# One list-schedule item for each marked group of small matmuls in a hybrid decoder layer

## The chip, the core and the metric

The kernel runs on one core of a Trainium2 chip. The metric is the device time of one execution in microseconds (us); a kernel's time is the median of its runs.

The engines are named as in the profile: PE is the matmul engine (PEld its weight loads), DVE, ACT and POOL are the vector, scalar and general engines, SP issues nearly all DMAs.

## The reference

One decoder layer over 4096 tokens of width 1024. The input is normalised and modulated, one projection feeds three mixers side by side, and their gated outputs go through one output projection:

```python
h = _rmsnorm(x, g_pre) * (1.0 + scale[:, None]) + shift[:, None]
proj = h @ w_in
...
attn = _sliding_window_attention(aq..., ak..., av..., sinks)   # 8 query heads, 2 kv heads, window 128
attn = attn * jax.nn.silu(ag)
...
rwkv = _rwkv7_mixer(h, rr, rk, rv, ...) * jax.nn.silu(rg)      # 4 heads of 64, delta-rule state per head
gla = _gla_mixer(h, gq, gkk, gv, gk1, gk2, gk_b, gla_norm_w) * jax.nn.silu(gg)   # 4 heads, key 32, value 64
y = jnp.concatenate([attn, rwkv, gla], axis=-1) @ w_out
return x + gate[:, None] * _rmsnorm(y, g_post)
```

RWKV and GLA are recurrences over the tokens, done in chunks: inside a chunk they are products of small matrices, and from chunk to chunk a state is carried.

## The kernel before

The 4096 tokens are cut into 16 slabs of 256. The program has two stages.

Stage one computes h, RWKV and GLA of all slabs, in generators that follow each slab: `a` (h), `p` (projections; their PSUM tiles are `pv`, `lp`, `zz`, `gqk`), `w` (decays and the a-lora `aps`), `qa` (RWKV scores: PSUM tiles `atp`, evacuated by DVE into `AT`), `qb` (scores go through DRAM, `adr`, into `AS`, and DVE solves small triangles step by step in `tsc` and `TT`), `qc` (small triangular products `Xp`, `Xq`, `X2`), `q2` (the RWKV state, four chunks one after the other: `rp`, `up`, `sp`, `yp`, then `yt`), `v`, `k` (transposes `kp`), `r` (GLA: scores `gap`, output `op`, state `kvp`) and `c` (weights split for stage two). Slab i+1 overlaps slab i, except where the state forces the order.

Stage two computes attention, gates and output projection of all slabs: `qkv` (`kp`, `qp`, `vp`), `gates` (`gp`), `s` (attention: scores `sc`, softmax on ACT and DVE, probabilities `pr` transposed on DVE, values `ovp`), `m` and `outp` (output projection, again tiles called `op`). A short stretch between the two stages (first slab's projections and attention) isn't ordered by hand.

Most matmuls use the whole 128x128 array. The small ones use a part of it and several can be in the array at once: 64x64 for `atp`, `gap`, `aps`, `rp`, `up` and half of `yp`, 128x64 for the GLA `op`, `sp` and the other half of `yp`, 32x64 for `ovp`, 32x32 for the triangles. The shape is called the tiling here. A matmul of fp32 data is two records of PE in the trace.

What sets the order: the generators run first only to record. A class `Order` notes every instruction (`note`) with the tiles that it reads and writes, and `pin` then simulates the engines with a table of costs, picks one ready instruction after the other and pins this order on each engine. A step becomes ready when the steps that it `needs` have ended, and those whose `turn` comes first (PSUM and SBUF buffers of one tag are handed out in the order of the program) have started. Among ready steps the lowest `rank` goes first (its place in the program); on PE a step of another tiling is passed over for up to `TILING_WAIT` when one of the present tiling is ready:

```python
            if e == "PE" and mode is not None and steps[k].array[0] != mode:

                same = [q for q in at if steps[q].array[0] == mode]
                wait = max(now - ready[e][q] for q in at if steps[q].array[0] != mode)
                if same and (mode != (4, 4) or wait < TILING_WAIT):
                    k = same[0]
```

So each matmul of a small product is an item of its own, and a product can be taken in pieces with other work between them.

PSUM has eight banks. The scores `atp` and `gap` use the banks of the tags `at` and `mq` (one buffer each), the GLA `op` uses `at`, the four `ovp` tiles use `tr`, `m`, `y` and `mq`.

All operations are issued through one helper, so that every instruction of the profile has its line: L320 in this kernel, L330 in the changed one, whose file is longer above it. Groups are told apart by their tiles.

Of the kernel before, what the change touches and what calls it, by code (L numbers as in the profile page):

```python
# [58 lines left out]
class Step:  # L59


    __slots__ = ("ins", "eng", "occ", "lat", "table", "array", "bytes", "half", "rank", "needs", "turn", "start", "end", "left", "then")


class Order:
# [1 line left out]


    def __init__(self, tc):
        self.tc, self.held, self.masks, self.lag, self.urgent = tc, {}, {}, 0, 0  # L70
        self.steps = []
        self.wrote, self.read, self.users, self.slots, self.known = {}, {}, {}, {}, set()

# [25 lines left out]
    def note(self, eng, name, outs, ins, func, r):  # L99

        st = Step()
        st.ins, st.eng, st.table, st.array, st.bytes, st.then = r.ins, str(eng.engine).split(".")[-1], None, None, 0, []
        st.half, st.rank = None, len(self.steps) + self.lag
        e, o = st.eng, outs[0]
        on_psum = [a for a in ins if str(a.tensor.space) == "PSUM"]
# [110 lines left out]
    def pin(self):  # L216

        steps = self.steps
        ready = {e: {} for e in ENGINES}
        for k, st in enumerate(steps):  # L220
            st.left = len(st.needs) + len(st.turn)
            for j in [*st.needs, *st.turn]:
                steps[j].then.append(k)
            if not st.left:
                ready[st.eng][k] = 0.0
        free = dict.fromkeys(ENGINES, 0.0)
        cells, mode, table, pipe, half = [0.0] * 16, None, None, 0.0, {}
        last = {}
        for _ in steps:
            e = min((e for e in ENGINES if ready[e]), key=lambda e: max(free[e], min(ready[e].values())))  # L230
            now = max(free[e], min(ready[e].values())) + 1e-9
            at = sorted((k for k, t in ready[e].items() if t <= now), key=lambda k: (steps[k].rank, k))
            k = at[0]
            if e == "PE" and mode is not None and steps[k].array[0] != mode:

                same = [q for q in at if steps[q].array[0] == mode]
                wait = max(now - ready[e][q] for q in at if steps[q].array[0] != mode)
                if same and (mode != (4, 4) or wait < TILING_WAIT):
                    k = same[0]
            st, t = steps[k], max(free[e], ready[e].pop(k))  # L240
            if e == "PE":
                m, at, passes, took, issue = st.array
                if mode is not None and m != mode:
                    t = max(t, max(cells)) + 0.094
                mode = m
                t = max(t, max(cells[c] for c in at))
                for c in at:
                    cells[c] = t + passes * took
                free[e], st.end = t + issue * passes, t + passes * took + 0.165
            else:  # L250
                if st.half is not None:
                    was, half[e] = half.get(e, st.half), st.half
                    if was[0] != st.half[0] or None not in (was[1], st.half[1]) and was[1] != st.half[1]:
                        t = max(t, free[e] + 0.115)
                if st.table is not None and st.table != table:
                    t, table = max(t, free[e] + 1.28), st.table
                free[e], st.end = t + st.occ, t + st.lat
                if st.bytes:

                    pipe = max(pipe, t + 1.7) + st.bytes / 310e3  # L260
                    st.end = max(st.end, pipe)
            st.start = t
            if e in last:
                self.tc.add_manual_dep(
                    st.ins, last[e], mybir.DependencyInfo(mybir.DependencyClass.NoSync, mybir.DependencyReason.DATA))
            last[e] = st.ins.name
            for q in st.then:
                to = steps[q]
                to.left -= 1
                if not to.left:  # L270
                    at = max([steps[j].start for j in to.turn], default=0.0)
                    for j, data in to.needs.items():
                        by = steps[j]
                        if by.eng != to.eng:
                            at = max(at, by.end + HOP_FROM[by.eng] + HOP_INTO.get(to.eng, 0.0))
                        elif to.eng == "SP":
                            at = max(at, by.end + 0.05)
                        elif to.eng != "PE" and data:
                            at = max(at, by.end + 0.03)
                    ready[to.eng][q] = at  # L280
        self.forget()


# [100 lines left out]
def hybrid_kernel(ctx, tc, x, vecs, rows, adaw, w1, wl, w2, wo, w2aug, a2, gk2, cst, ctr, ctg, abias, out):  # L384
# [92 lines left out]
    def mt(name):  # L477
        return pst("m", name)
# [43 lines left out]
            yield  # L522

    E = [dict() for _ in range(NS)]

# [98 lines left out]
    with ExitStack() as p1:  # L626
# [477 lines left out]
        def stage_d(i):  # L1104
# [39 lines left out]
            for b in range(2):  # L1144
# [4 lines left out]
                S.activation(em[:, b].rearrange("p c n -> p (c n)"), cw[:, :260], AF.Exp, scale=-1.0)  # L1149
                yield ["m"]  # L1150
            aps = mt("aps")
            for b in range(2):
                for h in range(2):
                    PE.matmul(aps[64 * h : 64 * h + 64, b * NT : (b + 1) * NT],
                              a2s[64:128, b * P + 64 * h : b * P + 64 * h + 64], x1[64:128, :], start=True, stop=True)
            ta = wt([P, 2, NT], "ta")
            e["ta"] = ta
            for b in range(2):
# [10 lines left out]
        def stage_qa(i):  # L1169
# [56 lines left out]
            corners = ((0, 0), (0, 1), (1, 0), (1, 1))  # L1226
            for g in range(2):
                aps_ = [pst(tag, "atp").rearrange("p (a b n) -> p a b n", a=2, b=2) for tag in ("at", "mq")]
                for c2 in range(2):
                    for b in range(2):  # L1230
                        for s, hb in corners:
                            c = 2 * g + c2
                            PE.matmul(aps_[hb][half[hb ^ s], c2, b, :], KB[half[hb], b, c, s, :],
                                      RA[half[hb], b, c].rearrange("p s n -> p (s n)"), start=(c2 == 0 and b == 0),
                                      stop=(c2 == 1 and b == 1))
                for hb in range(2):
                    V.tensor_tensor(AT[:, hb, 2 * g : 2 * g + 2], aps_[hb],
                                    rmask.rearrange("p (a b n) -> p a b n", a=1, b=1).to_broadcast([P, 2, 2, P]),
                                    op=ALU.mult)
                yield ["at", "mq"]  # L1240
# [101 lines left out]
        def stage_r(i):  # L1342
# [15 lines left out]
            for a in range(2):  # L1358
                yield [qb[a], "at", "mq"]
                gap = [pst(tag, "gap")[:, 0:NT] for tag in ("at", "mq")]  # L1360
                for hk in half:
                    for hp, sl in enumerate(half):
                        PE.matmul(gap[hp][hk], kg[sl, a, hk], qb[a][sl, 2 * hp : 2 * hp + 2, :].rearrange("p h n -> p (h n)"),
                                  start=True, stop=True)

                for hp in range(2):
                    V.tensor_tensor(qb[a][:, 2 * hp : 2 * hp + 2, :], gap[hp].rearrange("p (h n) -> p h n", h=2),
                                    gmask.rearrange("p (o n) -> p o n", o=1).to_broadcast([P, 2, P]), op=ALU.mult)
            yield [kt, "mq"]
            osb = wt([P, 2, NT], "osb", 1)  # L1370
            for a in range(2):
# [7 lines left out]
                V.scalar_tensor_tensor(Gn, Gn, egp[:, a, 128:129], bdm, op0=ALU.mult, op1=ALU.mult)  # L1379
                yield [Gc, qb[a], "at"]  # L1380
                op_ = pst("at", "op")
                for ht in half:
                    PE.matmul(op_[ht, :NT], qg[:, a, ht], Gc, start=True, stop=False)
                for h in range(4):
                    for ht in half:
                        PE.matmul(op_[ht, h * 64 : h * 64 + 64], qb[a][:, h, ht], vg[:, a, h * 64 : h * 64 + 64],
                                  start=False, stop=(h == 3))
                S.copy(osb[:, a, :], op_[:, :NT])
                yield [Gn, "mq"]
            osq = cs2([P, 2, NT], "osq")  # L1390
# [265 lines left out]
    def stage_s(i):  # L1656
# [8 lines left out]
        for a in range(2):  # L1665
# [48 lines left out]
            ov = [pst(tag, "ovp")[:, 0:P].rearrange("p (j n) -> p j n", j=4) for tag in tags]  # L1714

            lo = 4 if first else 0
            for d in range(5):
                for n in range(4):
                    if n + d < lo:
                        continue  # L1720
                    vt_, z = vblk[a + (n + d) // 4], (n + d) % 4
                    for kv in range(2):
                        PE.matmul(ov[n][kv * 64 : kv * 64 + 64], vt_[32 * n : 32 * n + 32, z, kv * 64 : kv * 64 + 64],
                                  pT[kv][32 * n : 32 * n + 32, :, 32 * (n + d) : 32 * (n + d) + 32],
                                  start=(n + d == max(lo, n)), stop=(d == 4))
            for n in range(4):
                S.copy(mx[:, 0:4, a * P + 32 * n : a * P + 32 * n + 32], ov[n])
            yield ["at", "sq"]
# [329 lines left out]
```

## Time and profile before

| | |
|---|---|
| runs | 2148.49, 2153.25, 2159.01 us; median 2153.25 |
| profiled execution | 2150.68 us, its span 2148.7 us, mean granted PE clock 0.985 |
| PE | 94% busy, 24311 matmul records |
| DVE | 76% busy, ACT 53%, POOL 9% |
| DMA | 241.90 MB, mean 113 GB/s |

Stage one ends at about 1120 us of the span, the stretch between the stages at about 1190 us, and stage two takes the rest. A busy PE in the page counts records that overlap, so the start of a record and the start of the next one tell more than their lengths.

### The profile page before, as it was taken

The numbers are of one execution on the slowest core, as the hardware profiler recorded it, in microseconds if no ns is written. First come the engines' busy times: TensorE is split into PE (matmuls) and PEld (weight loads), VectorE is DVE, ScalarE is ACT, GpSimd is POOL, SyncE is SP. The second block draws the span as 40 slices with busy tenths as digits, with TensorE's granted clock in tenths as the row PEclk, the third lists the DMA queues.
The fourth block names the chain that finished last, engine by engine and source line by source line (L and its number), as shares of the span: only waits on it lengthen the run. The fifth ranks groups of instructions, "written<-read, shape, count | busy, mean of one in ns | idle before, by whom it ended". The sixth has DMA issues, their size and how long they took to land. (4 is left out here: it accounts for less than half of the span.)

```text
span 2148.7 us, 60377 instructions
## 1 busy us (share of the span) xinstructions
PE 2025.3 (94%) x24311; PEld 1577.1 (73%) x24311; DVE 1630.7 (76%) x5204; ACT 1142.8 (53%) x2739; POOL 203.5 (9%) x404
## 2 busy tenths in 40 slices
PE   4999999999999999989888999999999999999996
PEld 4787788877787877777667667777777777777773
DVE  6687777678677789876765888777778877778876
ACT  3966676567776667654324444434344444444442
POOL 0010111111111111112600000000000000000000
PEclk9999999999999999999989999999999999999998
DMA  9232333133313224423415343433343333334341
GB/s 313 94 108 81 97 99 96 35 100 108 114 62 106 75 71 122 124 75 96 145 59 179 122 160 105 134 105 111 114 135 121 121 121 111 111 120 141 109 133 69
DMA packets 187249, 241.90 MB, mean 113 GB/s; under 512 B 52160, under 2 KB 145874, under 8 KB 182740
## 3 DMA queue, kind: packets, MB, share of 16 engines
q1 hardware_dynamic: 185220, 236.76, 34.4%
q8 instruction: 194, 3.18, 0.6%
q10 hardware_dynamic: 1744, 1.21, 0.2%
q14 instruction: 91, 0.75, 0.1%
HBM read 177.08 MB, written 60.82 MB: 111 GB/s over the span
## 5 line engine op out<-in xcount | busy, mean ns | idle before, releaser
L320 PEld LDWEIGHTS <-mtp 128*128 128x128 f16 x1344 | 130.8, 98 | 144.0 <-issue 5.3
L320 PE MATMUL op<-o,mtp 128*128 128x512 f16 x768 | 174.2, 380 | 0.0
L320 ACT ACTIVATE pr<-pr,nm,lsc 128x256 f32<-128x256 f32 (+1 forms) x256 | 149.7, 591 | 37.1 <-DVE nm L320 37.1
L320 PE MATMUL op<-ov,mtp 128*128 128x512 f16 x576 | 146.1, 383 | 2.3 <-ACT mtp L320 2.1
L320 PEld LDWEIGHTS <-hT 128*128 128x128 f16 x1536 | 116.6, 98 | 22.0 <-issue 4.2
L320 DVE TENSOR_TENSOR yv<-op,yv 128x512 f32<-128x512 f32 x112 | 75.3, 683 | 57.7 <-PE op L320 42.5
L320 DVE CUSTOM_DVE_ANT_0 pr<-sc,ab,sinks 128x256 f32<-128x256 f32 (+1 forms) x256 | 108.0, 476 | 14.4 <-PE sc L320 8.0
L320 ACT ACTIVATE mtp<-yv,oi 128x1024 f16<-128x1024 f32 x32 | 36.7, 1147 | 126.1 <-DVE yv L320 124.6
L320 ACT ACTIVATE ag<-gp,gh 128x512 f32<-128x512 f32 x64 | 43.7, 683 | 112.2 <-PE gp L320 112.2
L320 PE MATMUL pv<-gvh,hT 128*128 128x272 f16 x512 | 98.6, 282 | 1.1 <-DVE hT L320 1.0
L320 PE MATMUL gqk<-hT,gqkh 128*128 128x256 f16 x512 | 91.1, 277 | 4.8 <-DVE zb L320 4.8
L320 DVE SCALAR_TENSOR_TENSOR ag<-ag,gp 128x512 f32<-128x512 f32 x64 | 43.8, 684 | 68.1 <-ACT ag L320 68.1
L320 POOL COPY kT<-kT 128x512 f16<-128x512 f16 x15 | 9.9, 657 | 890.5 <-DVE kT L320 890.5
L320 PE MATMUL zz<-hT,kh 128*128 128x256 f16 x512 | 93.5, 273 | 0.0
L320 PE MATMUL qp<-hT,q1h 128*128 128x256 f16 x512 | 88.9, 278 | 4.0 <-DVE kT L320 4.0
L320 PE MATMUL lp<-hT,Lh 128*128 128x256 f16 x512 | 91.5, 276 | 0.4 <-ACT vg L320 0.2
L320 PE MATMUL zz<-hT,rh 128*128 128x256 f16 x512 | 90.1, 277 | 0.0
L320 PE MATMUL zz<-hT,vh 128*128 128x256 f16 x512 | 87.2, 273 | 0.8 <-DVE zb L320 0.8
L320 PE MATMUL gp<-hT,q3h 128*128 128x256 f16 x512 | 86.9, 274 | 0.1
L320 PE MATMUL qp<-hT,q0h 128*128 128x256 f16 x512 | 86.5, 275 | 0.4 <-DVE yv L320 0.4
L320 PE MATMUL gp<-hT,q5h 128*128 128x256 f16 x512 | 86.8, 273 | 0.0
L320 PE MATMUL gp<-hT,q4h 128*128 128x256 f16 x512 | 85.0, 273 | 0.0
(428 smaller groups left out, 6155.3 us busy)
## 6 DMA issues: line engine op xcount, KB each, us to landing
ov<-woscr SPq DMA_DIRECT2D x96, 512.0 KB, 4.3
xt<-in_x SPq DMA_DIRECT2D x16, 1024.0 KB, 5.1
hscr<-hT SPq DMA_DIRECT2D x16, 1024.0 KB, 5.5
hT<-hscr SPq DMA_DIRECT2D x16, 1024.0 KB, 4.8
out<-yv SPq DMA_DIRECT2D x32, 512.0 KB, 2.9
x<-in_x SPq DMA_DIRECT2D x30, 512.0 KB, 4.2
cs<-in_w SPq DMA_DIRECT2D x112, 128.0 KB, 2.3
v<-vscr SPq DMA_DIRECT2D x128, 64.0 KB, 3.4
```

Of the source, the lines that this page charges most:

```text
L320: r = f(*args, **kw)
```

## The change

The kernel marks five groups of matmuls with a number (`joint()` ... `joint(False)`): the a-lora `aps` (4 matmuls), each half of the RWKV scores `atp` (16), each half of the GLA scores `gap` (4), each GLA output `op` (10), and the attention values `ovp` (40). `note` stores the number in the step. In `pin`, neighbours on PE with one number and one tiling form a burst: its first member is its head, all outer needs and turns of the members count against the head, and when the head is picked all members are issued one behind the other. Everything else of `pin` keeps its rules (readiness is now summed as steps end, in `left` and `when`). No instruction of the program is added or taken away; the loads of ACT's function tables, which follow from the order, go from 65 to 67 in the built program.

```diff
+        bursts, head = {}, list(range(len(steps)))
         for k, st in enumerate(steps):
-            st.left = len(st.needs) + len(st.turn)
+            if st.eng == "PE":
+                h = head[k - 1] if k else 0
+                if k and steps[h].eng == "PE" and st.joint and st.joint == steps[h].joint and st.array[0] == steps[h].array[0]:
+                    head[k] = h
+                bursts.setdefault(head[k], []).append(k)
+        left, when = [0] * len(steps), [0.0] * len(steps)
+        for k, st in enumerate(steps):
             for j in [*st.needs, *st.turn]:
-                steps[j].then.append(k)
-            if not st.left:
+                if head[j] != head[k]:
+                    left[head[k]] += 1
+                    steps[j].then.append(k)
+        for k, st in enumerate(steps):
+            if head[k] == k and not left[k]:
                 ready[st.eng][k] = 0.0
...
-            st, t = steps[k], max(free[e], ready[e].pop(k))
-            if e == "PE":
...
+            first = max(free[e], ready[e].pop(k))
+            for k in bursts.get(k, [k]):
+                st, t = steps[k], max(first, free[e])
+                if e == "PE":
...
+    burst = itertools.count(1)
+
+    def joint(on=True):
+        model.order.joint = next(burst) if on else 0
...
             lo = 4 if first else 0
+            joint()
             for d in range(5):
...
                                   start=(n + d == max(lo, n)), stop=(d == 4))
+            joint(False)
```

How the order moves is shown at three places. The first is PE in stage two, within the gates of a slab (`gp` from the weights `q5h` and `q5l`): the attention values `ovp` of half a slab. In the kernel before, four of the 40 matmuls stand alone:

```order
L320 MATMUL gp<-hT,q5h 128x256
L320 MATMUL ovp<-pr,v_24378 64x128 x4
L320 LDWEIGHTS q5l
L320 MATMUL gp<-hT,q5l 128x256
L320 LDWEIGHTS q5h
```

and the other 36 follow seven `gp` matmuls later, again with `gp` on both sides:

```order
L320 LDWEIGHTS q5l
L320 MATMUL gp<-hT,q5l 128x256
L320 MATMUL ovp<-pr,v_24378 64x128 x10
L320 MATMUL ovp<-pr,v_24379 64x128 x2
L320 MATMUL ovp<-pr,v_24378 64x128 x4
L320 MATMUL ovp<-pr,v_24379 64x128 x4
L320 MATMUL ovp<-pr,v_24378 64x128 x2
L320 MATMUL ovp<-pr,v_24379 64x128 x14
L320 LDWEIGHTS q5h
```

In the changed kernel the same place in the slab has all 40 in a row:

```order
L330 LDWEIGHTS q5l
L330 MATMUL gp<-hT,q5l 128x256
L330 MATMUL ovp<-pr,v_24378 64x128 x14
L330 MATMUL ovp<-pr,v_24379 64x128 x2
L330 MATMUL ovp<-pr,v_24378 64x128 x4
L330 MATMUL ovp<-pr,v_24379 64x128 x4
L330 MATMUL ovp<-pr,v_24378 64x128 x2
L330 MATMUL ovp<-pr,v_24379 64x128 x14
L330 LDWEIGHTS q5h
```

One visit to the 32x64 tiling takes the place of two. All 30 groups of stage two that are scheduled so go the same way (60 visits before, 30 now, counted in both orders); the other half of each slab stands between `op` matmuls instead of `gp`, 14 of them after the `op` product began, as the larger piece did before.

The second place is PE in stage one, the RWKV scores of slab 13 (`atp_15749` and `atp_15750` are the two PSUM tiles of the first half, `zz` the projections of the next slab, `ktp` a transpose of GLA). Before, the first matmul of the group stood alone, early in the projection `zz_15889`:

```order
L320 MATMUL yp_15623<-UV_14110,AT_14207 64x64 x3
L320 MATMUL atp_15749<-RA_15652,KB_15651 64x128
L320 LDWEIGHTS kh_161
L320 MATMUL zz_15889<-hT_14662,kh_161 128x256
...
L320 MATMUL ktp_15733<-ident_63,kg_15296 128x128 x2
L320 LDWEIGHTS kh_161
L320 MATMUL zz_15889<-hT_14662,kh_161 128x256
L320 MATMUL atp_15749<-RA_15652,KB_15651 64x128 x7
L320 MATMUL atp_15750<-RA_15652,KB_15651 64x128 x8
```

Now the whole group stands in the projection after it, the two tiles by turns:

```order
L330 LDWEIGHTS rh_164
L330 MATMUL zz_16134<-hT_14662,rh_164 128x256
L330 MATMUL atp_15749<-RA_15652,KB_15651 64x128
L330 MATMUL atp_15750<-RA_15652,KB_15651 64x128
L330 MATMUL atp_15749<-RA_15652,KB_15651 64x128
```

Its last matmul is the 8331st of PE's matmul instructions before and the 8373rd now. Over stage one the changes of tiling in PE's order go from 619 to 613, since pieces of these groups mostly stood beside other matmuls of their tiling already; at the other slabs the groups move less.

The third place is SP's queue behind the scores of slab 13: `adr` takes them to DRAM in eight DMAs and `AS` fetches them for the solve; `a_18343` is the attention bias of stage two, `hscr` the store of h and `hf` a weight block. Before:

```order
L320 DMA adr<-AT 16x8x16 x8
L320 DMA hf<-in_adaw 128x4x128
L320 DMA a_18343<-in_abias 128x2048
L320 DMA hscr<-hT 128x4096
L320 DMA AS<-adr 64x256 x2
```

and in the changed kernel:

```order
L330 DMA a_18343<-in_abias 128x2048
L330 DMA hf<-in_adaw 128x4x128
L330 DMA hscr<-hT 128x4096
L330 DMA hf<-in_adaw 128x4x128
L330 DMA adr<-AT 16x8x16 x8
L330 DMA AS<-adr 64x256 x2
```

The three large transfers stand ahead of the scores now, and no longer between their store and their fetch. DVE's first step of that solve stands 10 DVE operations behind the last evacuation of `atp` now, and stood 21 behind it before.

More of the change, by code (lines that the diff above doesn't have):

```diff
@@ L59 @@
 class Step:
-    __slots__ = ("ins", "eng", "occ", "lat", "table", "array", "bytes", "half", "rank", "needs", "turn", "start", "end", "left", "then")
+    __slots__ = ("ins", "eng", "occ", "lat", "table", "array", "bytes", "half", "rank", "needs", "turn", "start", "end", "then", "joint")
 class Order:
     def __init__(self, tc):
-        self.tc, self.held, self.masks, self.lag, self.urgent = tc, {}, {}, 0, 0
+        self.tc, self.held, self.masks, self.lag, self.urgent, self.joint = tc, {}, {}, 0, 0, 0
         self.steps = []
@@ L102, in note @@
         st.ins, st.eng, st.table, st.array, st.bytes, st.then = r.ins, str(eng.engine).split(".")[-1], None, None, 0, []
+        st.joint = self.joint
         st.half, st.rank = None, len(self.steps) + self.lag
@@ L227, in pin @@
         cells, mode, table, pipe, half = [0.0] * 16, None, None, 0.0, {}
-        last = {}
-        for _ in steps:
+        last, count = {}, 0
+        while count < len(steps):
             e = min((e for e in ENGINES if ready[e]), key=lambda e: max(free[e], min(ready[e].values())))
@@ L239, in pin @@
                     k = same[0]
-            st, t = steps[k], max(free[e], ready[e].pop(k))
-            if e == "PE":
[L242 to L280, printed above, removed]
+            first = max(free[e], ready[e].pop(k))
@@ new lines, in pin @@
+            for k in bursts.get(k, [k]):
+                st, t = steps[k], max(first, free[e])
+                if e == "PE":
+                    m, at, passes, took, issue = st.array
+                    if mode is not None and m != mode:
+                        t = max(t, max(cells)) + 0.094
+                    mode = m
+                    t = max(t, max(cells[c] for c in at))
+                    for c in at:
+                        cells[c] = t + passes * took
+                    free[e], st.end = t + issue * passes, t + passes * took + 0.165
+                else:
+                    if st.half is not None:
+                        was, half[e] = half.get(e, st.half), st.half
+                        if was[0] != st.half[0] or None not in (was[1], st.half[1]) and was[1] != st.half[1]:
+                            t = max(t, free[e] + 0.115)
+                    if st.table is not None and st.table != table:
+                        t, table = max(t, free[e] + 1.28), st.table
+                    free[e], st.end = t + st.occ, t + st.lat
+                    if st.bytes:
+                        pipe = max(pipe, t + 1.7) + st.bytes / 310e3
+                        st.end = max(st.end, pipe)
+                st.start = t
+                if e in last:
+                    self.tc.add_manual_dep(
+                        st.ins, last[e], mybir.DependencyInfo(mybir.DependencyClass.NoSync, mybir.DependencyReason.DATA))
+                last[e], count = st.ins.name, count + 1
+                for q in st.then:
+                    to, h = steps[q], head[q]
+                    left[h] -= 1
+                    at = t if k in to.turn else 0.0
+                    if k in to.needs and e != to.eng:
+                        at = max(at, st.end + HOP_FROM[e] + HOP_INTO.get(to.eng, 0.0))
+                    elif k in to.needs and (e == "SP" or e != "PE" and to.needs[k]):
+                        at = max(at, st.end + (0.05 if e == "SP" else 0.03))
+                    when[h] = max(when[h], at)
+                    if not left[h]:
+                        ready[to.eng][h] = when[h]
@@ L1228, in stage_qa @@
                 aps_ = [pst(tag, "atp").rearrange("p (a b n) -> p a b n", a=2, b=2) for tag in ("at", "mq")]
+                joint()
                 for c2 in range(2):
@@ L1235, in stage_qa @@
                                       stop=(c2 == 1 and b == 1))
+                joint(False)
                 for hb in range(2):
@@ L1360, in stage_r @@
                 gap = [pst(tag, "gap")[:, 0:NT] for tag in ("at", "mq")]
+                joint()
                 for hk in half:
@@ L1364, in stage_r @@
                                   start=True, stop=True)
+                joint(False)
                 for hp in range(2):
@@ L1381, in stage_r @@
                 op_ = pst("at", "op")
+                joint()
                 for ht in half:
@@ L1387, in stage_r @@
                                   start=False, stop=(h == 3))
+                joint(False)
                 S.copy(osb[:, a, :], op_[:, :NT])
@@ L1716, in stage_s @@
             lo = 4 if first else 0
+            joint()
             for d in range(5):
@@ L1725, in stage_s @@
                                   start=(n + d == max(lo, n)), stop=(d == 4))
+            joint(False)
             for n in range(4):
```

## The prediction

> **What bounds the kernel now.** I read the page's first part, then busy time by stretches, then PE's waits in each stretch. The page:
>
> ```profile
> PE 2025.3 (94%) x24311; PEld 1577.1 (73%) x24311; DVE 1630.7 (76%) x5204; ACT 1142.8 (53%) x2739; POOL 203.5 (9%) x404
> ```
>
> PE leads, but records overlap, so the share alone proves little. Busy time by stretch (from and to, length, then busy us and records of PE, PEld, DVE, ACT and POOL, the granted PE clock, DMA's share and GB/s):
>
> ```profile
> 100.00:940.00 840.00, 816.31 (x11640) 663.66 (x11638) 660.44 (x2371) 570.00 (x1345) 129.40 (x271) 1.00 0.31 93
> 940.00:1040.00 100.00, 88.59 (x1148) 71.31 (x1148) 66.20 (x243) 41.56 (x94) 31.29 (x55) 0.95 0.34 105
> 1040.00:1130.00 90.00, 78.34 (x1270) 58.86 (x1269) 60.59 (x208) 25.78 (x57) 29.13 (x42) 0.92 0.33 99
> 1130.00:1195.00 65.00, 54.50 (x574) 45.58 (x572) 40.89 (x125) 28.76 (x82) 0.70 (x1) 0.92 0.50 162
> 1200.00:2100.00 900.00, 886.31 (x9017) 661.32 (x9016) 704.45 (x1950) 402.37 (x1021) 8.55 (x13) 1.00 0.37 122
> ```
>
> Stage one to 940 us and stage two have PE covered to 97% and 98% at full clock. From 940 to 1195 us (end of stage one and the stretch between) PE is free for 88.59, 78.34 and 54.50 of 100, 90 and 65 us: chains through other engines decide there. What PE waits for in stage two (first query) and from 940 to 1040 us (second):
>
> ```profile
> PE sc L320 <- DVE m L320: 12.9, 14, 1.4
> ...
> PE gqk L320 <- DVE zb L320: 4.1, 1, 4.1
> PE ot L320 <- DVE osb L320: 3.6, 1, 3.6
> ```
>
> In stage two there is one wait per slab, scores for DVE, and nothing else of size. So what shortens PE's own work in stage two shortens the kernel, as long as that wait doesn't grow.
>
> **Attention values in stage two: two visits become one.** In the timeline of PE (start us, length), a slab's gates with the two pieces of `ovp`:
>
> ```profile
> 1335.12 0.38 PE L320 MATMUL gp<-hT,q5h 128*128 128x256 f16 x2
> 1335.43 0.45 PE L320 MATMUL ovp<-pr,v 32*64 32x128 f32 x8
> 1335.81 0.28 PE L320 MATMUL gp<-hT,q5l 128*128 128x256 f16 x1
> ...
> 1336.15 0.27 PE L320 MATMUL gp<-hT,q5l 128*128 128x256 f16 x1
> 1336.26 0.38 PE L320 MATMUL gp<-hT,q5h 128*128 128x256 f16 x2
> 1336.48 0.27 PE L320 MATMUL gp<-hT,q5l 128*128 128x256 f16 x1
> 1336.68 1.41 PE L320 MATMUL ovp<-pr,v 32*64 32x128 f32 x72
> 1338.02 0.39 PE L320 MATMUL gp<-hT,q5h 128*128 128x256 f16 x2
> ```
>
> Three `gp` from 1336.15 to 1336.48 make 0.11 us from start to start. The last `gp` ahead of the first piece thus starts at 1335.23, and the next at 1335.81: 0.58, of which 0.11 is its own, so the visit costs 0.47. The second costs 1338.02 - 1336.48 - 0.11 = 1.43. Together 1.90. For the joint group I take the entry (1336.68 - 1336.48 = 0.20), the 1.34 that 72 records and the exit take (1336.68 to 1338.02), and eight more records at (1.34 - 0.38) / 64 = 0.015 each, 0.12: 0.20 + 1.34 + 0.12 - 0.11 = 1.55. Saved: 0.35 per group.
>
> The bounds. One group was issued whole already, in the unscheduled stretch:
>
> ```profile
> 1155.80 0.42 PE L320 MATMUL qp<-hT,q1h 128*128 128x256 f16 x1
> 1156.01 0.42 PE L320 MATMUL qp<-hT,q1l 128*128 128x256 f16 x1
> 1156.36 1.66 PE L320 MATMUL ovp<-pr,v 32*64 32x128 f32 x80
> 1157.95 0.39 PE L320 MATMUL qp<-hT,q1h 128*128 128x256 f16 x2
> ```
>
> From 1156.36 to 1157.95 it took 1.59, so 0.20 + 1.59 - 0.11 = 1.68 and 0.22 saved; but it began at low clock (the `qp` ahead of it start 0.21 apart, not 0.11), so this is the worst end. At best the eight ride in gaps of the 72: 0.20 + 1.34 - 0.11 = 1.43, 0.47 saved. With 30 groups the term is **-10.5 us, from -6.6 to -14.1**. That nothing of it goes through the rest of a group: two records per matmul and 80 per group,
>
> ```profile
> L320 PE MATMUL ovp<-pr,v x2520: 264/268/471, 1138.7 to 2099.1; 32*64 32x128 f32 x194
> ```
>
> are 2400 of 2520 for 30 groups, the rest lies in the unscheduled stretch.
>
> The Trainium skill (TensorEngine Tiling (Array Packing), Key Properties) says that a change of tiling mode drains the array. The trace shows less than a full record: 0.20 from the start of a `gp` to the start of `ovp`, where a lone `gp` record lasts 0.27. With 0.27 at both ends of a removed visit the term would be an estimate of 30 x (0.35 + 0.14) = 14.7 instead of 10.5.
>
> Is the joint group late? It needs both transposes of `pr`. In the other half of the slab, where the pieces stand between `op`:
>
> ```profile
> 1379.21 1.24 DVE L320 STREAM_TRANSPOSE pr<-pr 128x1024 f32<-128x1024 f32 x1
> 1380.37 1.25 DVE L320 TENSOR_TENSOR yv<-op,yv 128x512 f32<-128x512 f32 x2
> 1381.54 1.23 DVE L320 STREAM_TRANSPOSE pr<-pr 128x1024 f32<-128x1024 f32 x1
> ...
> 1381.67 0.45 PE L320 MATMUL ovp<-pr,v 32*64 32x128 f32 x8
> ...
> 1383.67 1.41 PE L320 MATMUL ovp<-pr,v 32*64 32x128 f32 x72
> ```
>
> The second transpose ends at 1382.77. The group stands where the larger piece stood, and PE gets there 0.47 sooner, at 1383.20: 0.43 to spare. That is the cover; without it PE would wait for the difference. The scores that follow stand two `op` later than before, so DVE has no less time for them. The wait of scores for DVE (12.9 us in 14 slabs) follows a DVE chain that PE's own earlier work of the slab sets off, so it moves along and keeps its size.
>
> **The groups of stage one.** Pieces stood mostly beside matmuls of their tiling, so only six changes of tiling go. What a visit costs there, at slab 13's scores:
>
> ```profile
> 929.00 0.43 PE L320 MATMUL atp<-RA,KB 64*64 64x128 f32 x2
> 929.36 0.39 PE L320 MATMUL zz<-hT,kh 128*128 128x256 f16 x2
> ...
> 930.07 0.27 PE L320 MATMUL zz<-hT,kh 128*128 128x256 f16 x1
> 930.27 1.59 PE L320 MATMUL atp<-RA,KB 64*64 64x128 f32 x24
> ```
>
> 0.20 on the way in (930.07 to 930.27), about as much on the way out, less a pitch of 0.11: 0.3 a visit, three visits fewer, **-0.9 us**. That the groups now wait for all their members costs nothing up to 940 us, since PE takes projections meanwhile (816.31 of 840 us busy); if that cover fails, PE waits for the last member.
>
> At the end the cover is thin. Slab 13's scores end 42 matmul instructions later in PE's order. At 14 records per us (11640 in 840 us) and one or two records each, this is 3 to 6 us; every later link of slab 13 (solve, triangles, state) hangs on it. Against it stands the SP queue: before, DVE waited for `AS`,
>
> ```profile
> DVE tsc L320 <- POOL AS L320: 5.2, 1, 5.2
> ```
>
> which I put down to its place behind the bias and h in SP's queue; now it follows its store directly, so the 5.2 may go. I set the two against each other, 0, with -5.2 and +6 as bounds.
>
> ACT gets two more table loads from the new order:
>
> ```profile
> L320 ACT ACT_TABLE_LOAD x63 | 80.8, 1283 | 5.3 <-DMA sinks<-in_rows 4.2
> ```
>
> at 1.28 us each. ACT is busy for 53% of the span, so I cost them at nothing; with that cover gone it were 2.6.
>
> **Sum.** -10.5 - 0.9 + 0 = -11.4 us. The profiled execution took 2150.68 us (span 2148.7), which gives 2139.3; the profiled execution lies 2.6 below the median of the runs, 2153.25, and against that the forecast is **2141.8 us**, from 2153.25 - 14.1 - 0.9 - 5.2 = 2133 to 2153.25 - 6.6 - 0.9 + 6 = 2152. A measurement of this kernel can tell about 0.5%, 10.8 us, from no change: faster is under 2142.5, slower over 2164.0.
>
> **Rivals.**
>
> *The end of stage one gives it back.* The late scores of slabs 13 to 15 add up instead of being caught up, and the chain that fills 940 to 1195 us starts later by 6 us or somewhat more. For it: PE has 33.6 us of idle time in those 255 us, so PE work no longer sets the time there. Against it: the end of the queue wait. Price: +6 to +11, total 2148 to 2153; no change.
>
> *DVE stalls in line.* DVE takes its instructions in order. Now only 10 operations stand between scores and the solve's first step, instead of 21, so DVE may reach that step sooner than `AS` lands and stand still with everything queued behind it (state updates, evacuations of `zz`), for which PE waits as at `gqk` (4.1). If the 5.2 of slab 13 grows to 10 and recurs at slabs 14 and 15 and in a few others, about 35 us more are lost: 2153.25 - 11.4 + 35 = 2177, slower. It decides for slower once new stalls on the path exceed 22 us. Against it: the scores land faster now. What a long wait does to the clock, from the same waits at 1130 to 1195 us:
>
> ```profile
> PE qp L320 <- DVE kT L320: 4.0, 1, 4.0
> ```
>
> After it the `qp` records start 0.21 apart instead of 0.11. The Trainium skill (TensorE: Matmul & The Clock Gate, Part 1) holds that an idle window of about 3.4 us halves PE's clock until PE has been busy as long; the trace agrees, and by an estimate each such stall would cost up to 1.7 us more.
>
> *Nothing is saved in stage two,* because DVE's chain sets the pace and the wait at the scores grows by what the visits lose: only the -0.9 is left, 2152, no change. Against it: in 900 us DVE works 704.45.
>
> **How the numbers follow.** Forecast 0.62 (0.46 of it under 2142.5, since the threshold lies close beside the sum, 0.16 within 0.5%); end of stage one 0.22; DVE stalls 0.10; nothing saved 0.06. Faster 0.46, same 0.44, slower 0.10. The range takes in the forecast's bounds, most of the first rival and 3 us for the runs' own spread below: 2130 to 2157.
>
> **What would show it.** Right: in stage two 30 rows of `ovp` with x80, about 1.46 from their start to the next `op` or `gp`, the period of a slab shorter by 0.7, the scores' wait still about 12.9 in 14; stage two reaching its steady state at the same time as before within 6 us. Wrong: a wait of `ovp` for `pr`, a larger wait of `sc` for `m`, or stage two starting more than 10 us later, with DVE waits for `AS`.

## The result and the profile after

The changed kernel takes 2123.16 us (median, 2121.01 to 2124.73) against 2150.87 us (2147.79 to 2159.01) of the kernel before on the same chip: ratio 0.9865, interval 0.9834 to 0.9895. In a second comparison it was 0.9883 (0.9859 to 0.9908). The forecast, 2141.8 in 2130 to 2157, had the sign right and the size wrong: 28 us were saved, not 11, and the time lies below the range.

The page's first part after:

```profile
span 2121.6 us, 60360 instructions
PE 1997.8 (94%) x24311; PEld 1567.6 (74%) x24311; DVE 1616.1 (76%) x5204; ACT 1142.4 (54%) x2741; POOL 207.6 (10%) x404
```

PE does the same 24311 records, busy 27.5 us less (2025.3 before), about as much as the span lost (2148.7 to 2121.6). Where along the span? Two tiles mark the places: `yt` closes a slab of stage one, `ovp` ends stage two. The rows by tile give the count, min/median/max ns, first and last start; for each tile, before first and then after:

```profile
L320 PE MATMUL yt<-ident,ysb x64: 272/273/474, 198.2 to 1122.9; 128*128 128x128 f32 x64
```

```profile
L330 PE MATMUL yt<-ident,ysb x64: 272/273/476, 197.2 to 1109.8; 128*128 128x128 f32 x64
L330 PE MATMUL ovp<-pr,v x2520: 267/268/318, 1125.2 to 2072.1; 32*64 32x128 f32 x194
```

The last `yt` starts 13.1 us earlier, the first `ovp` 13.5 (1138.7 before) and the last `ovp` 27.0 (2099.1 before). So half was gained in stage one and half in stage two. Stage one's lead grew up to slab 9 (they count from 0), whose last `yt` starts 11.2 us earlier, and little behind it. The window view (length, busy us and records by engine, granted PE clock, DMA share, GB/s), after:

```profile
100.00:940.00 840.00, 816.41 (x11784) 665.34 (x11784) 656.28 (x2387) 573.69 (x1357) 137.41 (x277) 1.00 0.32 97
940.00:1200.00 260.00, 226.64 (x3004) 177.84 (x3004) 173.00 (x599) 100.09 (x245) 57.52 (x92) 0.92 0.37 114
```

By 940 us PE has done 144 records more than before (11640), at 13.9 records per us 10 us of lead. Those are the 840 us in which I had forecast almost nothing (-0.9 us).

What changed there, in the timeline of PE (start, length). Before, half a GLA score group (`gap`) on its own, and a score group of RWKV (`atp`) in two pieces:

```profile
362.60 0.27 PE L320 MATMUL zz<-hT,kl 128*128 128x256 f16 x1
362.80 0.65 PE L320 MATMUL gap<-qb,kg 64*64 64x256 f32 x4
363.38 0.39 PE L320 MATMUL zz<-hT,kh 128*128 128x256 f16 x2
...
419.02 0.43 PE L320 MATMUL atp<-RA,KB 64*64 64x128 f32 x4
419.39 0.28 PE L320 MATMUL lp<-hT,Ll 128*128 128x256 f16 x1
...
420.15 1.09 PE L320 MATMUL atp<-RA,KB 64*64 64x128 f32 x28
421.07 0.33 PE L320 MATMUL rp<-UV,AT 64*64 64x64 f32 x5
```

After, the same groups whole:

```profile
364.44 0.27 PE L330 MATMUL zz<-hT,kl 128*128 128x256 f16 x1
364.65 0.66 PE L330 MATMUL gap<-qb,kg 64*64 64x256 f32 x8
365.24 0.33 PE L330 MATMUL yp<-UV,AT 128*64 128x64 f32 x2
...
413.06 1.10 PE L330 MATMUL atp<-RA,KB 64*64 64x128 f32 x32
414.00 0.33 PE L330 MATMUL rp<-UV,AT 64*64 64x64 f32 x5
```

Read starts, not lengths. Half a `gap` group holds PE for 363.38 - 362.80 = 0.58 us, a whole one for 365.24 - 364.65 = 0.59. 28 records of `atp` take 0.92, all 32 take 0.94, and the four alone took 0.37 more. This isn't the price of a change of tiling alone: 16 half groups of `gap` went in one piece in the kernel before and took 0.56 to 0.69 us, and eight of them began directly behind other 64x64 matmuls. I matched every record with PE's order and summed, for each piece, the time from its start to the start of what follows: all `gap` groups went from 29.7 us in 61 pieces to 20.1 in 32, `atp` from 40.8 us in 47 pieces to 33.1 in 32. That is 17.3 us of PE's own time; `op` (34.1 to 35.3) and `aps` (13.9 to 15.8) gained nothing. I call this the own time of a group below.

Stage two shows the same thing in the group whose rows before the prediction quotes:

```profile
1320.53 0.38 PE L330 MATMUL gp<-hT,q5h 128*128 128x256 f16 x2
1320.75 0.27 PE L330 MATMUL gp<-hT,q5l 128*128 128x256 f16 x1
1320.95 1.43 PE L330 MATMUL ovp<-pr,v 32*64 32x128 f32 x80
1322.32 0.39 PE L330 MATMUL gp<-hT,q5h 128*128 128x256 f16 x2
```

80 records take 1.37 from start to next start where 72 took 1.34: eight more cost 0.03, not 0.12. The waits of stage two (total, times, longest) stayed:

```profile
PE sc L330 <- DVE m L330: 13.1, 14, 1.4
PE mp L330 <- ACT mtp L330: 3.5, 1, 3.5
PE op L330 <- ACT mtp L330: 2.1, 1, 2.1
```

### The profile page after: what moved, and what is told of

It reads as the page before. It is cut to its first block, busy times and chain, and to the rows that moved or that the text cites. A ratio compares the mean times of both kernels' runs of the same rounds, so it can differ in the third digit from the quotient of the medians.

```text
span 2121.6 us, 60360 instructions
## 1 busy us (share of the span) xinstructions
PE 1997.8 (94%) x24311; PEld 1567.6 (74%) x24311; DVE 1616.1 (76%) x5204; ACT 1142.4 (54%) x2741; POOL 207.6 (10%) x404
## 5 line engine op out<-in xcount | busy, mean ns | idle before, releaser
L330 DVE SCALAR_TENSOR_TENSOR ag<-ag,gp 128x512 f32<-128x512 f32 x64 | 43.8, 684 | 58.9 <-ACT ag L330 58.5
L330 ACT ACT_TABLE_LOAD x65 | 83.4, 1283 | 5.2 <-DMA sinks<-in_rows 4.1
```

The source lines that it names most:

```text
L330: r = f(*args, **kw)
```

## Experiments

All ratios are against the kernel before, run on the same chip; it took 2148 to 2151 us in every set. Records are those of PE between 100 and 940 us (11640 before).

| kernel | ratio | interval | records |
|---|---|---|---|
| all five marks, again | 0.9883 | 0.9859 to 0.9908 | 11770 |
| `ovp` alone | 0.9945 | 0.9926 to 0.9964 | 11639 |
| `atp` alone | 0.9962 | 0.9949 to 0.9975 | 11762 |
| `gap` alone | 0.9996 | 0.9982 to 1.0009 | 11633 |
| `op` alone | 0.9984 | 0.9966 to 1.0002 | 11596 |
| `atp` and `gap` | 0.9958 | 0.9942 to 0.9974 | 11753 |
| all but `gap` | 0.9934 | 0.9909 to 0.9960 | 11668 |
| all but `op`, `aps` | 0.9914 | 0.9894 to 0.9935 | 11785 |
| before's order, pieces joined afterwards | 1.0015 | 0.9999 to 1.0030 | 11477 |
| RWKV and GLA scores tile by tile | 0.9911 | 0.9892 to 0.9930 | 11699 |
| `ovp` in the old inner order | 0.9875 | 0.9852 to 0.9899 | 11773 |
| TILING_WAIT 0.3 | 0.9899 | 0.9874 to 0.9923 | 11823 |
| TILING_WAIT 0.45 | 0.9907 | 0.9880 to 0.9935 | 11796 |
| TILING_WAIT 0.8 | 1.0002 | 0.9984 to 1.0020 | 11628 |
| TILING_WAIT 1.0 | 1.0023 | 1.0008 to 1.0039 | 11562 |
| TILING_WAIT 2.5 | 1.0508 | 1.0474 to 1.0542 | 10333 |

### One mark at a time

The edit is the same for each: the `joint()` pairs of the other groups go.

```diff
-                joint()
...
-                joint(False)
```

Attention values alone:

> Only the attention values (ovp) are issued as joint groups; stage one is ordered as before. Theory A (own time): each visit and each half-filled visit to the array costs PE time, and the groups' gains add up; stage two's share of the change is all here: 30 groups x 0.47 less 2, so 11 to 13 us under before, stage two's slab period 0.9 shorter, stage one's end within 1 us of before. Theory B (new order): stage two gains as much, so the same 11 to 13 us; the rest of the 27 us of the change comes from the new order of stage one as a whole. If stage two only gains behind an earlier end of stage one, this run shows less than 8 us.

Measured 0.9945, 11.8 us less. Stage two's half of the result is this mark's, and it needs no earlier end of stage one (the last `yt` starts at 1121.8 here, 1122.9 before).

RWKV scores alone:

> Only RWKV's scores (atp) are issued as joint groups. Theory A: the two PSUM tiles are taken by turns in every group (0.84 us from first record to last instead of up to 1.2) and no visit holds one matmul alone; own time falls by 6 to 8 us, the entries by 4, the kernel gains 5 to 10 us. Theory B: within 4 us of before or slower, unrelated to the groups' own time.

Measured 0.9962, 8.2 us less; own time 40.8 to 31.9 us. Theory A's figure. In this profile the last `yt` starts 11.1 us earlier than before, most of what all five marks gain there:

```profile
L330 PE MATMUL yt<-ident,ysb x64: 272/273/474, 197.3 to 1111.8; 128*128 128x128 f32 x64
```

GLA scores alone:

> Only GLA's scores (gap) are issued as joint groups. Theory A: a piece of two matmuls uses one row half of the array and costs as much as the whole group of four; the groups' own time falls by about 9 us (from start to the next item) and their entries by 2 to 3; PE being the bound up to 940 us, the kernel gains 6 to 12 us, the gain growing slab by slab. Theory B: the stage-one gain belongs to one arrangement of the whole schedule, so this kernel lands anywhere, within 4 us of before or slower, and not in step with the groups' own time.

Measured 0.9996: nothing. The own time of `gap` fell as expected, 29.7 to 19.5 us, but the kernel didn't follow. `atp` was now cut into 52 pieces instead of 47 (own time 40.8 to 43.8), and a wait came up that before did not have in this size (waits of PE from 100 to 940 us):

```profile
PE atp L330 <- DVE RA L330: 3.4, 3, 2.8
```

Before, the longest of that kind was 0.6. So theory A falls in its simple form: a group's own time isn't the kernel's time. The scheduler rearranges everything behind the group; which part of that used up the gain isn't shown.

GLA output alone:

> Only the GLA output (op) is joint; the a-lora is marked as well, which moves nothing since its four matmuls were whole before. The same sum over neighbours gives 4.5 us less in stage one than before (8.0 less with atp alone, 0.3 more with gap alone). Theory A (fewer pieces and visits): 2 to 7 us under before. Theory B (the mark is worth something only through the end of stage one with the others): within 2 us of before.

Measured 0.9984, 3.4 us, with an interval that reaches 1: unclear between the two.

### The old order held, pieces joined in it

`pin` schedules as before and keeps each engine's row; then, before the rows are pinned:

```diff
+            for end in (max(spots), min(spots)):
+                mark = pe[end]
+                rest = [k for k in pe if k not in g or k == mark]
+                n = rest.index(mark)
+                trial = dict(row, PE=rest[:n] + sorted(g) + rest[n + 1:])
```

> The schedule of before is kept on all engines; afterwards the pieces of a marked group are brought together on PE at the place of its last (or first) member, wherever that leaves no circle of waits: all 30 ovp groups, 9 of the op groups that were in pieces (41 pieces to 32), 9 of the split atp groups (47 pieces to 37) and 14 of the split gap groups (61 pieces to 47). Nothing else moves. Theory A: 12 us from ovp, about half of gap's 12 and two thirds of atp's 12, in all 20 to 27 us under before. Theory B: only the 12 us of ovp, since stage one keeps its old order.

Measured 1.0015, missed by both theories. Stage two kept its gain (first to last `ovp` 946.8 us, 960.3 before), so stage one lost about as much: the last `yt` starts 10.1 us later, and PE is 163 records behind at 940 us, busy 7.7 us less up to there (808.62 instead of 816.31). For part of it PE stands ahead of the joined groups, waiting for members whose data aren't there yet (waits from 100 to 940 us):

```profile
PE gap L368 <- ACT kt L368: 2.4, 2, 2.1
PE gap L368 <- DVE qb L368: 1.3, 2, 0.7
PE gap L368 <- DVE AT L368: 0.7, 1, 0.7
```

Before, the one wait of `gap` was 0.3. The three come to 4.4 us; the rest is spread over other waits. In stage two joining pays in the old order too; in stage one it cost, and every gain there was seen with a schedule that was made again around the joint item.

### What a piece costs: the order inside a group

In both kernels the changed kernel's order is held and only the places of a group's members among themselves are exchanged, after the scheduler has run.

Scores tile by tile:

```diff
+        name = [self.steps[k].to.tensor.name for k in g]
+        if not any(x in name[0] for x in ("atp", "gap")):
+            return g
+        return [k for own in dict.fromkeys(name) for k, x in zip(g, name) if x == own]
```

> The changed kernel with one edit: within each joint group of RWKV scores and GLA scores the matmuls of one PSUM tile (one row half of the array) come first, then those of the other, instead of by turns; the rest of the order is held. Theory A (the row halves work side by side only when they are taken by turns): a gap group is longer by 0.25 to 0.3 us, an atp group by 0.35 or more, 32 of each, so stage one is 15 to 25 us longer. Theory B (only visits and the schedule count): within 3 us of the changed kernel.

Measured 2129.64 us against 2125.06 of the changed kernel in the same set, 4.6 us more; 71 records fewer by 940 us (11699 against 11770). `atp` behaves as theory A says: own time 34.0 to 44.0 us, 0.31 per group, though no visit was added. `gap` doesn't: 20.1 to 19.6. Its four matmuls lie on four different parts of the array (64 rows by 64 columns each) whichever comes first, while an `atp` group visits each of its four parts four times, so tile by tile its matmuls use only two parts at a time. Of the 10 us of PE time, half reached the end. The expectation of 15 to 25 had both wrong: the price of `gap`, and that own time is kernel time.

`ovp` in the old inner order:

```diff
+        if len(g) != 40:
+            return g
+        return g[0:8:2] + g[1:8:2] + g[8:]
```

> The changed kernel with one edit: within each of the 30 joint ovp groups the four matmuls that stood alone before (first layer, column half 0) go ahead of the four of column half 64, as in the old order, but with nothing between them; the rest of the order is held. Theory A (half-filled layers): half a layer costs what a whole one does, so the group is longer by 0.1 to 0.15 us, 1.55 instead of 1.43, and stage two by 3 to 4.5 us. Theory B (only the entry and the exit of a visit cost): no difference, within 1 us in stage two.

Measured 0.9875, 2122.62 us, no loss. The group's own time is the same in both orders, 1.37 us. Theory A falls: the order of the first eight matmuls costs nothing as long as nothing stands between them. For these groups the runs don't tell whether the price of the old split was the second entry and exit or the interruption of these eight itself.

### Marks left out

> The changed kernel again, beside before on the same chip and beside the kernels below. If the whole is more than its parts (values of attention alone 0.9945, RWKV scores alone 0.9962, GLA scores alone 0.9996, together 0.9903), it comes out at 0.985 to 0.988 again, 25 to 32 us under before; if the parts add up, at 0.990.

Measured 0.9883. The product of the single ratios (0.9945, 0.9962, 0.9996, 0.9984) is 0.9887, so here the parts add up. This is no rule: without `gap`'s mark (below) the product is 0.9891, and 0.9934 is measured.

> The marks of the GLA output (op) and the a-lora (aps) are taken away, the other three stay. The own time of op and aps did not fall in the changed kernel (34.1 to 35.3 and 13.9 to 15.8 us), so by their own time the marks bring nothing: within 4 us of the changed kernel, on either side. If the order that they lead to is what saves stage one's 13 us, this kernel loses 6 us or more against the changed one.

Measured 0.9914, 6.2 us slower than the changed kernel. By 940 us it is level (11785 records); it loses behind that, most of it in the last slab (ahead of the kernel before by 12.2 us at slab 14's last `yt` and by 7.7 at slab 15's).

> The changed kernel without the marks of the GLA scores (gap). The gap groups' own time fell by 9.6 us in the changed kernel, but alone the mark changed nothing. Theory A1 (the gain is spent at once: fewer gap pieces mean more pieces of atp and new waits, whatever else is marked): within 4 us of the changed kernel. Theory A2 (alone it was lost only because atp was then cut into more pieces; with atp joint that can't happen): 6 to 10 us slower than the changed kernel. Summing, for each pair of neighbours in PE's order, the median start-to-start time of such a pair in the trace of before gives no difference between the two, which speaks for A1.

Measured 0.9934 against 0.9883 for all five, some 11 us slower: nearer to A2 than to A1. At 940 us it is already 102 records behind the changed kernel, and in its profile nothing is left of stage one's gain, although `atp` is joint:

```profile
L330 PE MATMUL yt<-ident,ysb x64: 272/273/473, 198.4 to 1122.5; 128*128 128x128 f32 x64
```

> Only RWKV's and GLA's scores are joint. If gap's mark needs atp's, stage one up to slab 12 is 13 us shorter than before, as it was with the attention values joint on top (7.8 with atp alone), and what of it reaches the end depends on the last slabs: 6 to 14 us under before. If gap's gain came from op's mark instead, it is like atp alone, 6 to 10 us under, with no more than 8 us up to slab 12.

Measured 0.9958, like `atp` alone (0.9962), and 11753 records against 11762. So `gap` gained nothing beside `atp` either, which speaks against A2's reason, and the total lies in both expectations. The mark is worth 0, 0 and 11 us in three surroundings. About half of the 11 us may be a loss that comes up where `op` and `aps` are marked beside `atp` and `gap` isn't: 0.9934 (0.9909 to 0.9960) stands against 0.9907, the product of `atp` and `ovp` alone, some 6 us at the edge of the interval. Why the marks act on each other so, the runs don't settle. The same stage-one order (all but `op` and `aps`, this kernel) differed by 32 records, 2 us, between two profiles, and by 5.2 us at slab 12's last `yt`, which is too little to explain it.

### Fewer visits by waiting longer

The profile's lesson seemed to be: fewer visits. The scheduler has a constant for that.

```diff
-TILING_WAIT = 0.6
+TILING_WAIT = 1.0
```

> The changed kernel with TILING_WAIT 1.0 instead of 0.6: an item of the full array is passed over longer while one of the present tiling is ready, and 601 instead of 613 changes of tiling are left in stage one, 61 instead of 60 in stage two. The sum over neighbours is 8 us less in stage one and 2 us more in stage two. If visits and pieces are what counts, it is 3 to 8 us under the changed kernel; if the delayed projections feed the chains that DVE works on, it is equal or slower.

> The same with TILING_WAIT 2.5: 572 changes of tiling in stage one, 60 in stage two; the sum over neighbours is 3 us less than in the changed kernel. If visits alone count (41 fewer at 0.2 to 0.3 us), 8 to 12 us under the changed kernel; if waits for delayed projections are added, slower than it.

> The same with TILING_WAIT 0.8: 611 changes of tiling in stage one, 61 in stage two, the sum over neighbours 0.3 us more in stage one and 2 us more in stage two. If the loss at 1.0 grows with the wait, this lies between: 5 to 20 us over the changed kernel; if it is a matter of one unlucky place, within 4 us of the changed kernel.

> The same with TILING_WAIT 0.45: 610 changes of tiling in stage one, the sum over neighbours 3 us less than in the changed kernel. Both fewer visits and a shorter wait: 0 to 6 us under the changed kernel by either theory; if slower, the arrangement of the last slabs decides, and not the rule.

> The changed kernel with TILING_WAIT 0.3 instead of 0.6, so items of the full array are passed over for less long: 621 instead of 613 changes of tiling in stage one, 60 in stage two as before. The sum over neighbours is 2 us more. If visits count alone, 2 to 4 us slower than the changed kernel; if waiting in line is the dearer side already at 0.6, equal or faster.

Below 0.6 nothing is gained: 0.3 is within the noise of the changed kernel, and 0.45, expected 0 to 6 us under it, came out some 5 over. 0.8, expected 5 to 20 over, loses the whole gain of the change, some 25, and 2.5 costs 5%. At 1.0 the changes of tiling fall by 12, and the recurrence pays for it (last `yt`, and the stretch from 940 us):

```profile
L330 PE MATMUL yt<-ident,ysb x64: 272/273/477, 196.7 to 1149.0; 128*128 128x128 f32 x64
...
940.00:1200.00 260.00, 209.90 (x2903) 166.20 (x2904) 160.19 (x564) 89.68 (x218) 60.49 (x98) 0.87 0.33 98
```

The last `yt` starts at 1149.0, 39 us after the changed kernel's 1109.8, and PE is busy for 209.90 of 260 us there instead of 226.64. I expected 3 to 8 us less by counting visits; slower, as the other branch said, is what came. Its reason, delayed work on the chains, fits the idle PE and isn't shown further. Counting visits alone fails here as it failed in the prediction. None of the five waits beat the changed kernel.

## Why the prediction missed

- **"The groups of stage one", the step that failed.** It counted changes of tiling, six fewer at 0.3, and wrote -0.9. Measured -13.1 at the last `yt`. What it left out stands in rows of the kernel before: a piece beside other matmuls of its tiling needs no change of tiling, but a half `gap` group takes 0.58 us there too, where a whole one takes 0.59. 29 pieces of `gap` and 15 of `atp` went, 17.3 us of PE's own time. `atp` alone gave 8.2; the tile-by-tile kernel, which adds no visit, shows that such a cost of `atp` reaches the end at about half. For `gap` the way from 9.6 us of own time to the kernel's time isn't settled: alone and beside `atp` it brought nothing. How much of the 17.3 us arrives depends on the schedule as a whole. "Costs nothing up to 940 us" was right as far as waits go: `atp` waits for `RA` 0.2 us instead of 1.9.
- **Attention values, right and a little small.** -10.5 within -6.6 to -14.1; alone 11.8. The joint group costs 1322.32 - 1320.75 - 0.11 = 1.46, not 1.55: the eight extra records cost 0.03, close to my "best" bound of riding along. That is 0.44 saved per group and 13.2 for 30, and the stretch from the first to the last `ovp` is 13.5 shorter. The drain estimate of 14.7 lies above all of these. `ovp` waits for nothing in stage two, and the scores' wait for DVE moved along, 12.9 to 13.1 us.
- **End of stage one, right.** The forecast was 0 in -5.2 to +6. From the last `yt` to the first `ovp` the lead went from 13.1 to 13.5. Both sides of the sum came. Slab 13's scores lose part of the lead: the last `atp` record starts 10.1 us earlier than before at slab 12, 7.3 at slab 13 (926.9, 934.2 before). In return their fetch lands sooner, as the new order in SP's queue would have it. Slab 13's took 9.3 us from issue to landing before, the slowest of all, and now none takes more than 3.2 (rows of `AS`, before first and then after):

```profile
DMA to landing us min/median/max: 2.1/2.2/9.3
```

```profile
DMA to landing us min/median/max: 2.1/2.3/3.2
```

So slab 13's solve starts 12.5 us sooner:

```profile
951.36 0.18 DVE L320 TENSOR_TENSOR tsc<-TT,AS 128x16 f32<-128x16 f32 x1 [5.21 <-POOL AS L320]
```

```profile
938.88 0.18 DVE L330 TENSOR_TENSOR tsc<-TT,AS 128x16 f32<-128x16 f32 x1 [3.62 <-POOL AS L330]
```

The wait of 5.2 us itself didn't go, as the prediction thought it might. DVE comes to the step sooner too, and stands there for 3.6 us.

- **ACT's table loads, right.** 65 in the trace, 83.4 us instead of 80.8, with ACT busy for 54%; no wait shown above is put down to them.
- **The rivals.** "DVE stalls in line" hardly came: DVE waits for `AS` ten times instead of six in stage one, but 9.7 us in all instead of 8.2, and the longest wait got shorter (3.6). "The end gives it back" didn't come for this arrangement, but all marks but `op` and `aps` lost some 6 us, most of it there, so the risk was real. "Nothing is saved in stage two" is refuted by the `ovp` run.
- **The range** added bounds of the terms I had. The term with the wrong base (visits instead of own time) entered them as a fixed -0.9, so the low end of 2130 fell 7 us short.

## What to carry to other kernels

Price a group of small matmuls by what it occupies from its start to the next start, for the pieces and for the whole; if half costs as much as all, as with `gap` here, a cut costs a whole group, even beside matmuls of the same tiling. Then let the scheduler plan with the joint item: joining in a fixed order lost in stage one what it saved in stage two, and delaying other work to make visits rarer lost more than it saved. And don't take the own time that is saved for the kernel's time: between none and nearly all of it reached the end here.

## What was unexpected in the hardware

- Two of four 64x64 matmuls of 256 fp32 columns (`gap`) hold PE for 0.58 us, all four for 0.59; 28 records of 64x64 by 128 columns take 0.92, 32 take 0.94; 72 records of 32x64 take 1.34, 80 take 1.37.
- The order of the four `gap` matmuls didn't matter (20.1 and 19.6 us for all groups), that of sixteen `atp` matmuls did (34.0 and 44.0): using two of four parts of the array at a time costs 0.31 us per group.
